# One PSUM tile for all ragged ends: v, k and K tails gathered before a joint transpose, and one sample-output product for both heads

## The chip, the core and the metric

The kernel runs on one core of a Trainium2 chip. The metric is the device time of one execution in microseconds (us). Five engines work side by side, each through its own instructions in order: TensorE (PE in the profile; PEld is its weight load), VectorE (DVE), ScalarE (ACT), GpSimd (POOL) and SyncE (SP), which here issues most of the DMA transfers. They wait for each other by semaphores.

## What is computed

One layer of a decoder: a feed-forward block, a token mixer and a second feed-forward block. 16 meta tokens and 256 prompt tokens (one sequence of 272) and 8 sample tokens (one step of eight independent sequences, each with a state of its own) go through the same weights, so an activation here is a matrix of 280 columns. The mixer, cut to what matters:

```python
q_r, k_r, v_r, g_r, q_h, f_h, i_h, g_h, a_r, a_h = jnp.split(x @ w_in, N_PROJ, axis=-1)
...
# retention, 8 heads of 256 x 256, decay gamma per head
inner = jnp.einsum('bhid,bhjd->bhij', q, k) * D
S_new = jnp.exp(lg * C)[:, None, None] * S + jnp.einsum('bhjd,bhjv->bhdv', k_dec, v)
...
# HGRN2, 16 heads of 128 x 128, gate f per channel, k = 1 - f
A = jnp.einsum('bhid,bhjd,bhijd->bhij', q, k, decay)
o = jnp.einsum('bhij,bhjv->bhiv', A, v) + jnp.einsum('bhid,bhdv->bhiv', q * jnp.exp(b), S)
```

The outputs are y of the prompt and the samples, and both kinds of state after the prompt and after each sample's step.

## The kernel before

Activations lie transposed: 128 channels on the partitions, tokens along the free axis (16 meta, 256 prompt, 8 sample). A product in float32 accuracy is made of three passes in a reduced format: `dense` multiplies the high part of the weights by the high and the low part of x, and the low part of the weights by the high part of x. A weight block of 128x1024 is loaded (`raw`), cast on ACT (`whi`, L187) and subtracted on DVE (`wlo`, L188). The dense matmuls are all L217 in the profile.

The mixer stands between the two feed-forward blocks, from about 780 to 1760 us. It goes through eight units (u = 0 to 7), each with one retention head and two HGRN2 heads, about 130 us for a unit. `project` runs the dense products of `w_in` for the unit's ten projections. After each contraction step it calls `pump`, which advances two generators, `mix_hg` and `mix_ret`. They hold the mixer's own work, cut into steps by `yield n` (come again after n dense steps). TensorE's order is therefore written out by hand: a step's small matmuls stand between dense matmuls, and a matmul whose operand isn't ready holds all dense matmuls behind it. On ACT, DVE and SP a scheduler orders the instructions by priority and estimate. Mixer products take their PSUM bank from a ring of four (`mx_bank`).

The 280 tokens don't fit blocks of 128. Where an operand is needed with tokens on the partitions, it is transposed on TensorE in three pieces, two of 128 tokens and a ragged one. In `mix_ret` (L978 on) the ragged piece has 24 tokens: the prompt's last 16 and the 8 samples. For each half c of the 256 channels, the bank `pt` first takes the three transposes of v (L997). ACT copies out the two whole blocks (`vt`, called vtr in the profile, L998) and the ragged rows (`vt2`, L999). `split` makes the high and low parts `vs`, and `upper_lower_upper` (L705) makes from `vt2` the tile `vs2`: high, low and high parts, 32 rows each, so that one 128-row product does the three passes of the ragged rows. A second bank `pt` takes the transposes of k (L1006), scaled by the decay on ACT (L1011) into `ks` and for the ragged rows into `ks2` (twice), with the low parts subtracted on DVE (L1012). Then the scores `psc` (L1024) follow and, for each c, the prompt state `psr` (L1041): six matmuls of `vs` with `ks`, and as the seventh `vs2` with `ks2`. The profile drops a digit at the end of a name: vs2 and ks2 appear there as vs and ks with 24 rows, vt2 as vt with 24 rows.

The sample rows of `vt2` also leave by a DMA to memory (`vrd`, L720) and come back spread over all partitions (`vbr`, L1055), for the update of the sample states `smr` (L1061).

In `mix_hg` the ragged piece of K is the 16 meta tokens, transposed for each head h into the third part of the bank `ptk` (L899) and split into `km`. The sample outputs of HGRN2 are products of 32 rows each (`pq`, L932), 128 columns for each head. Their result goes through `osh` (L936) and is transposed back per head in `sample_columns` (L727). `alone` (L723) spreads the samples' q columns so that each stands alone in a block of 32 columns.

Of the kernel before, what the change touches and what calls it, by code (L numbers as in the profile page):

```python
# [18 lines left out]
P = 128  # L19
# [31 lines left out]

SCORES = ((0, 0, SEQ, P), (SEQ, P - NMETA, 2 * P - P + NMETA, P), (2 * SEQ - P + NMETA, SEQ - NMETA, NMETA, LP - 2 * P))
# [75 lines left out]
def trunk(ctx: ExitStack, tc: tile.TileContext, A, O):  # L128
# [124 lines left out]
    def sub(out, a, b):  # L253
        nc.vector.tensor_tensor(out=out, in0=a, in1=b, op=ALU.subtract)
# [291 lines left out]
    with tc.tile_pool(name="yp", bufs=1) as yp:  # L546
# [7 lines left out]
        with tc.tile_pool(name="mp", bufs=1) as mp:  # L554
# [33 lines left out]
            qdh = tmp("qdh", (P, 2, NS * 32))  # L588
            qdr = tmp("qdr", (P, 2, NS * 32))
            nc.gpsimd.memset(qdh, 0.0)  # L590
            nc.gpsimd.memset(qdr, 0.0)
            vsm = tmp("vsm", (P, P))
# [8 lines left out]
            sc2 = tmp("sc2", (P, NMETA), dt=F32R)  # L601
            for z in (km, vm, ks2, vs2, sc2):
                z = z if len(z.shape) == 2 else z.rearrange("p c f -> p (c f)")
                nc.scalar.copy(z, qdh[:, 0, : z.shape[1]])
# [106 lines left out]
            def upper_upper_lower(out, x):  # L711
                n = x.shape[0]
                nc.scalar.copy(out[:n], x)
                nc.scalar.copy(out[32 : 32 + n], x)
                sub(out[64 : 64 + n], x, out[:n].bitcast(F32))
# [7 lines left out]
            def alone(qd, q):  # L723
                for e in range(2):
                    nc.vector.tensor_copy(qd[:, :, 128 * e + e : 128 * e + 128 : 32], q[:, :, SEQ + 4 * e : SEQ + 4 * e + 4])

            def sample_columns(on, po, os):  # L727

                nc.tensor.transpose(po[:, 3 * P :], os, ident)
                nc.vector.tensor_copy(  # L730
                    on[:, SEQ:].rearrange("p (e j) -> p e j", e=2), po[:, 3 * P :].rearrange("p (j c) -> p c j", c=32)[:, 0:2, :])

            def mix_hg(u, f, k, q, v):
# [60 lines left out]
                for s in LEVELS:  # L794
# [59 lines left out]
                    if s == 2:  # L854
# [12 lines left out]
                            t4.unsqueeze(3).to_broadcast([P, 2, 16, 8]))  # L867
                    if s in (4, 8):
# [25 lines left out]
                for h in range(2):  # L894
                    kt = tmp("kth", (P, 2, P), bufs=2)
                    kts.append(kt)
                    pt = mx_bank("ptk")
                    for b, (t0, n) in enumerate(((NMETA, P), (NMETA + P, P), (0, NMETA))):
                        nc.tensor.transpose(pt[:n, b * P : (b + 1) * P], K[:, h, t0 : t0 + n], ident)  # L899
                    nc.scalar.copy(kt, pt[:, : 2 * P].rearrange("p (b f) -> p b f", b=2))  # L900
                    upper_upper_lower(km[:, h, :], pt[:NMETA, 2 * P : 3 * P])

                    vb, sm = vbs[h], sms[h]
                    for b in range(NS):
                        nc.scalar.activation(sm[:, b, :], sm[:, b, :], AF.Copy, scale=fk[:, 0, h, b : b + 1])
                        nc.vector.scalar_tensor_tensor(
                            out=sm[:, b, :], in0=vb[:, b, :], scalar=fk[:, 1, h, b : b + 1], in1=sm[:, b, :],
                            op0=ALU.mult, op1=ALU.add)
                    nc.sync.dma_start(O["sgs"][2 * u + h], sm)
                    yield 2  # L910
# [18 lines left out]
                for h in range(2):  # L929
                    for b in range(NS):  # L930
                        j = 32 * (b % 4)
                        nc.tensor.matmul(  # L932
                            pq[j : j + 32, h * P : (h + 1) * P], qdh[:, h, 32 * b : 32 * b + 32], sms[h][:, b, :],
                            start=b < 4, stop=b >= 4, tile_position=(0, j))
                os = tmp("osh", (P, 2 * P))
                nc.scalar.copy(os, pq[:, : 2 * P])  # L936
                yield 4

                def outputs(h):
# [5 lines left out]
                    sample_columns(on[:, h, :], po, os[:, h * P : (h + 1) * P])  # L945
# [31 lines left out]
            def mix_ret(u, q, k, v):  # L977
# [15 lines left out]
                nc.sync.dma_start(dt, A["dtab"][u])  # L993
                for c in range(2):
                    pt = mx_bank("pt")
                    for b, (t0, n) in enumerate(BLOCKS):
                        nc.tensor.transpose(pt[:n, b * P : (b + 1) * P], v[:, c, t0 : t0 + n], ident)  # L997
                    nc.scalar.copy(vt[:, :, c, :], pt[:, : 2 * P].rearrange("p (b f) -> p b f", b=2))  # L998
                    nc.scalar.copy(vt2[:NB, c, :], pt[:NB, 2 * P : 3 * P])  # L999
                    f = slice(c * P, (c + 1) * P)  # L1000
                    split(vs[:, 0, :, f], vs[:, 1, :, f], vt[:, :, c, :])
                    upper_lower_upper(vs2[:, c, :], vt2[:NB, c, :])
                    yield 1
                    pt = mx_bank("pt")
                    for b, (t0, n) in enumerate(BLOCKS):
                        nc.tensor.transpose(pt[:n, b * P : (b + 1) * P], k[:, c, t0 : t0 + n], ident)  # L1006
                    for b, (t0, n) in enumerate(BLOCKS):
                        x, g = pt[:n, b * P : (b + 1) * P], dec[:n, b, u : u + 1]
                        his = [ks[:, 0, b, f]] if b < 2 else [ks2[third[0], c, :], ks2[third[1], c, :]]
                        for hi in his:  # L1010
                            nc.scalar.activation(hi, x, AF.Copy, scale=g)  # L1011
                        nc.vector.scalar_tensor_tensor(  # L1012
                            out=(ks[:, 1, b, f] if b < 2 else ks2[third[2], c, :]), in0=x, scalar=g,
                            in1=his[0].bitcast(F32), op0=ALU.mult, op1=ALU.subtract)
# [54 lines left out]
                for e in range(2):  # L1069
                    for c in range(2):  # L1070
                        for j in range(4):
                            b = 4 * e + j
                            nc.tensor.matmul(
                                pq[32 * j : 32 * j + 32, :256], qdr[:, c, 32 * b : 32 * b + 32],
# [10 lines left out]
                for c in range(2):  # L1085
# [3 lines left out]
                    sample_columns(on[:, c, :], po, os[:, c * P : (c + 1) * P])  # L1089
# [149 lines left out]
```

## Time and profile before

| what | value |
|---|---|
| time, median of 3 runs | 2612.75 us (2611.18 to 2614.51) |
| time of the profiled execution | 2606.34 us |
| its span | 2604.6 us |
| TensorE busy | 99% of the span |
| VectorE, ScalarE, GpSimd busy | 66%, 53%, 0% |
| mean share of the DMA engines, unit u=3 (1140 to 1270 us) | 0.71 |

The profiled execution was 6.4 us under the median of the runs. Between its own time and its span lie 1.74 us. Rows of the trace give the start in us from the start of the span, the duration in us, the engine, the line, the operation, the tiles (output before input) and in brackets the idle time ahead with what ended it. "x3" is three instructions taken as one row. Matmuls are pipelined, so a row's duration is longer than the step from one start to the next, and the step is what a matmul costs.

### The profile page before, as it was taken

Reading aid. Unit: us, or ns where it says so; the run is one execution under the profiler, and the core shown is the slowest. Engines: PE = TensorE matmul, PEld = TensorE weight load, DVE = VectorE, ACT = ScalarE, POOL = GpSimd, SP = SyncE. Lnnn points to the kernel's source line nnn. Section 1 sums busy time; section 2 is a strip of 40 time slices with the busy share of each in tenths; the row PEclk is TensorE's granted clock in tenths of the full one; section 3 lists DMA queues with packets and bytes.
Section 4 is the critical chain, followed back from the end, with each engine's and each line's share of the span. In section 5 each row is a group of like instructions: output and inputs, shape, how many; then the busy total and the mean of one; then the engine's idle time right before and its main releaser. Section 6 shows DMA issues by size and latency. Waiting matters only on the chain.

```text
span 2604.6 us, 54857 instructions
## 1 busy us (share of the span) xinstructions
PE 2581.1 (99%) x22744; PEld 2553.0 (98%) x22744; DVE 1721.4 (66%) x2907; ACT 1380.7 (53%) x2184; POOL 12.1 (0%) x54
## 2 busy tenths in 40 slices
PE   9999999999999999999999999999999999999998
PEld 9999999999999999999999999999999999999998
DVE  6454445565579788777878787776995555556555
ACT  5444444444466667756666666574564444444443
POOL 0000000000000000000000000000000000000000
PEclk9999999999999999999999999999999999999999
DMA  7555555555566686767676767665656566656664
GB/s 243 184 185 186 184 182 186 186 181 184 186 198 217 227 271 211 251 214 248 219 244 213 250 218 244 205 233 194 188 191 198 195 197 196 197 195 194 195 195 147
DMA packets 154586, 536.17 MB, mean 206 GB/s; under 512 B 17696, under 2 KB 25696, under 8 KB 154336
## 3 DMA queue, kind: packets, MB, share of 16 engines
q1 hardware_dynamic: 154048, 532.37, 62.5%
q8 instruction: 178, 2.92, 0.5%
q14 instruction: 72, 0.59, 0.1%
q10 hardware_dynamic: 288, 0.29, 0.1%
HBM read 501.99 MB, written 30.61 MB: 204 GB/s over the span
## 4 chain that ended last, share of the span: by engine, by line
PE 91%; DVE 4%; DMA 2%; ACT 2%; issue 1%; SPq 0%; DVEq 0%; ACTq 0%
PE up L217 36%; PE dn L217 18%; PE wo L217 3%; PE pj_f L217 3%; PE pj_q_h L217 3%; PE pj_g_r L217 3%; PE pj_k_r L217 3%; PE pj_a_r L217 3%; PE pj_v_r L217 3%; PE pj_i_h L217 3%; PE pj_q_r L217 3%; PE pj_g_h L217 3%; PE pj_a_h L217 2%; DVE wlo L188 1%; DMA smr<-in_sr 1%
## 5 line engine op out<-in xcount | busy, mean ns | idle before, releaser
L188 DVE TENSOR_TENSOR wlo<-raw,whi 128x1024 fp32r<-128x1024 f32 (+1 forms) x869 | 1062.6, 1224 | 734.2 <-ACT whi L187 732.4
L187 ACT CAST whi<-raw 128x1024 fp32r<-128x1024 f32 (+1 forms) x870 | 904.9, 1042 | 890.2 <-PE up L217 416.9
L217 PE MATMUL up<-xh,wlo 128*128 128x280 f32 (+1 forms) x2624 | 725.8, 280 | 0.4 <-DVE wlo L188 0.3
L217 PE MATMUL up<-xh,whi 128*128 128x280 f32 (+1 forms) x2624 | 725.7, 280 | 0.5 <-ACT whi L187 0.5
L217 PE MATMUL up<-xl,whi 128*128 128x280 f32 (+1 forms) x2624 | 725.4, 279 | 0.0
L217 PEld LDWEIGHTS up<-xh,wlo 128*128 128x128 f32 x2624 | 492.5, 189 | 1.0 <-DVE wlo L188 1.0
L217 PEld LDWEIGHTS up<-xh,whi 128*128 128x128 f32 x2624 | 492.6, 189 | 0.9 <-ACT whi L187 0.8
L217 PEld LDWEIGHTS up<-xl,whi 128*128 128x128 f32 x2624 | 492.6, 189 | 0.0
L217 PE MATMUL dn<-hh,whi 128*128 128x280 f32 (+1 forms) x1376 | 384.7, 280 | 0.0
L217 PE MATMUL dn<-hh,wlo 128*128 128x280 f32 (+1 forms) x1376 | 384.3, 279 | 0.0
L217 PE MATMUL dn<-hl,whi 128*128 128x280 f32 (+1 forms) x1376 | 384.3, 279 | 0.0
L217 PEld LDWEIGHTS dn<-hh,whi 128*128 128x128 f32 x1376 | 260.1, 189 | 0.1
L217 PEld LDWEIGHTS dn<-hl,whi 128*128 128x128 f32 x1376 | 260.1, 189 | 0.1
L217 PEld LDWEIGHTS dn<-hh,wlo 128*128 128x128 f32 x1376 | 260.1, 189 | 0.0
L217 PE MATMUL pj_g_r<-xh,whi 128*128 128x264 f32 x256 | 76.7, 299 | 0.0
L217 PE MATMUL pj_g_h<-xh,wlo 128*128 128x264 f32 x256 | 71.3, 278 | 3.2 <-DVE wlo L188 3.2
L217 PE MATMUL pj_v_r<-xh,whi 128*128 128x280 f32 x256 | 74.2, 290 | 0.0
L217 PE MATMUL pj_g_h<-xh,whi 128*128 128x264 f32 x256 | 73.6, 287 | 0.0
L217 PE MATMUL pj_k_r<-xh,wlo 128*128 128x280 f32 x256 | 72.6, 283 | 0.2 <-DVE wlo L188 0.2
L217 PE MATMUL pj_v_r<-xh,wlo 128*128 128x280 f32 x256 | 72.4, 283 | 0.3 <-DVE wlo L188 0.3
L217 PE MATMUL pj_k_r<-xh,whi 128*128 128x280 f32 x256 | 72.7, 284 | 0.0
L217 PE MATMUL pj_v_r<-xl,whi 128*128 128x280 f32 x256 | 72.3, 283 | 0.0
(402 smaller groups left out, 5277.6 us busy)
## 6 DMA issues: line engine op xcount, KB each, us to landing
raw<-in_w_up SPq DMA_DIRECT2D x343, 512.0 KB, 3.4
raw<-in_w_in SPq DMA_DIRECT2D x320, 512.0 KB, 3.9
raw<-in_w_dn SPq DMA_DIRECT2D x172, 512.0 KB, 3.6
smr<-in_sr SPq DMA_DIRECT2D x32, 512.0 KB, 5.6
out_srs<-smr SPq DMA_DIRECT2D x32, 512.0 KB, 5.1
raw<-in_w_out SPq DMA_DIRECT2D x32, 512.0 KB, 3.7
smh<-in_sg SPq DMA_DIRECT2D x16, 512.0 KB, 4.2
vbr<-vrd SPq DMA_DIRECT2D x16, 512.0 KB, 4.2
```

The source lines that it names most:

```text
L187: nc.scalar.copy(hi[:, j:jn, :], raw[:, j:jn, :])
L188: nc.vector.tensor_tensor(out=lo[:, j0:j1, :], in0=raw[:, j0:j1, :], in1=hi[:, j0:j1, :].bitcast(F32), op=ALU.subtract)
L217: nc.tensor.matmul(o, w, t, start=start, stop=stop)
```

## The change

The ragged pieces are gathered before they are transposed. GpSimd copies the 24 ragged columns of k and of v, two channel halves each, into one tile `tails` (four groups of 32 columns), and the 16 meta columns of both heads' K into `meta` (two groups of 32). One transpose of `tails` goes into the third part of the bank `pt` of k's first half, and one transpose of `meta` into the bank `ptk` of the first head. In the first, rows 0 to 63 are k and rows 64 to 127 are v: `ks2`, `vt2` and `vs2` for both channel halves are now all read from this one bank. In HGRN2 the sample products of the second head accumulate onto those of the first, in the same 128 columns: the q columns of each sample stand in their own row of the 32, which `alone` now writes with one copy in place of two. `osh` is half as wide, and one transpose and one copy serve both heads.

```diff
+ALONE = 4 * 32 + 1
 SCORES = ((0, 0, SEQ, P), (SEQ, P - NMETA, 2 * P - P + NMETA, P), (2 * SEQ - P + NMETA, SEQ - NMETA, NMETA, LP - 2 * P))
...
-            qdh = tmp("qdh", (P, 2, NS * 32))
-            qdr = tmp("qdr", (P, 2, NS * 32))
+            qdh = tmp("qdh", (P, 4, ALONE))
+            qdr = tmp("qdr", (P, 4, ALONE))
             nc.gpsimd.memset(qdh, 0.0)
             nc.gpsimd.memset(qdr, 0.0)
+            qdh_at = [qdh.rearrange("p a c -> p (a c)")[:, 256 * h :] for h in range(2)]
+            qdr_at = [qdr.rearrange("p a c -> p (a c)")[:, 2 * ALONE * c :] for c in range(2)]
             vsm = tmp("vsm", (P, P))
...
             sc2 = tmp("sc2", (P, NMETA), dt=F32R)
+            tails = tmp("tails", (P, 4, 32))
+            meta = tmp("meta", (P, 2, 32))
+            nc.gpsimd.memset(tails, 0.0)
+            nc.gpsimd.memset(meta, 0.0)
+            dec2 = tmp("dec2", (P, HR))
+            for i in range(2):
+                nc.scalar.copy(dec2[32 * i : 32 * i + T - 2 * P], dec[: T - 2 * P, 2, :])
             for z in (km, vm, ks2, vs2, sc2):
                 z = z if len(z.shape) == 2 else z.rearrange("p c f -> p (c f)")
-                nc.scalar.copy(z, qdh[:, 0, : z.shape[1]])
+                nc.scalar.copy(z, qdh_at[0][:, : z.shape[1]])
             threads = []
...
-            def upper_upper_lower(out, x):
+            def upper_upper_lower(out, x, at=0):
                 n = x.shape[0]
...
                 nc.scalar.copy(out[32 : 32 + n], x)
-                sub(out[64 : 64 + n], x, out[:n].bitcast(F32))
+                sub(out[64 : 64 + n], x, out[at : at + n].bitcast(F32))
...
             def alone(qd, q):
-                for e in range(2):
-                    nc.vector.tensor_copy(qd[:, :, 128 * e + e : 128 * e + 128 : 32], q[:, :, SEQ + 4 * e : SEQ + 4 * e + 4])
+                nc.vector.tensor_copy(
+                    qd[:, :, : 128 : 32].rearrange("p (c e) j -> p c e j", e=2),
+                    q[:, :, SEQ:].rearrange("p c (e j) -> p c e j", e=2))
             def sample_columns(on, po, os):
+                n = on.shape[1]
                 nc.tensor.transpose(po[:, 3 * P :], os, ident)
                 nc.vector.tensor_copy(
-                    on[:, SEQ:].rearrange("p (e j) -> p e j", e=2), po[:, 3 * P :].rearrange("p (j c) -> p c j", c=32)[:, 0:2, :])
+                    on[:, :, SEQ:].rearrange("p h (e j) -> p h e j", e=2),
+                    po[:, 3 * P :].rearrange("p (j c) -> p c j", c=32)[:, : 2 * n, :].rearrange("p (h e) j -> p h e j", e=2))
             def mix_hg(u, f, k, q, v):
...
                             t4.unsqueeze(3).to_broadcast([P, 2, 16, 8]))
+                    if s == 8:
+                        nc.gpsimd.tensor_copy(meta[:, :, :NMETA], K[:, :, :NMETA])
                     if s in (4, 8):
...
                     pt = mx_bank("ptk")
-                    for b, (t0, n) in enumerate(((NMETA, P), (NMETA + P, P), (0, NMETA))):
-                        nc.tensor.transpose(pt[:n, b * P : (b + 1) * P], K[:, h, t0 : t0 + n], ident)
+                    for b in range(2):
+                        t0 = NMETA + b * P
+                        nc.tensor.transpose(pt[:, b * P : (b + 1) * P], K[:, h, t0 : t0 + P], ident)
+                    x = pt[:64, 2 * P : 3 * P]
+                    if h == 0:
+                        nc.tensor.transpose(x, meta.rearrange("p h t -> p (h t)"), ident)
+                        for i in range(2):
+                            upper_upper_lower(km[:, i, :], x[32 * i : 32 * i + NMETA], 32 * i)
                     nc.scalar.copy(kt, pt[:, : 2 * P].rearrange("p (b f) -> p b f", b=2))
-                    upper_upper_lower(km[:, h, :], pt[:NMETA, 2 * P : 3 * P])
...
                         nc.tensor.matmul(
-                            pq[j : j + 32, h * P : (h + 1) * P], qdh[:, h, 32 * b : 32 * b + 32], sms[h][:, b, :],
-                            start=b < 4, stop=b >= 4, tile_position=(0, j))
-                os = tmp("osh", (P, 2 * P))
-                nc.scalar.copy(os, pq[:, : 2 * P])
+                            pq[j : j + 32, :P], qdh_at[h][:, 32 * b : 32 * b + 32], sms[h][:, b, :],
+                            start=h == 0 and b < 4, stop=h == 1 and b >= 4, tile_position=(0, j))
+                os = tmp("osh", (P, P))
+                nc.scalar.copy(os, pq[:, :P])
                 yield 4
...
                         nc.tensor.matmul(o, Ss[h][:, b, :], Q[:, h, b * P : (b + 1) * P], start=False, stop=True)
-                    sample_columns(on[:, h, :], po, os[:, h * P : (h + 1) * P])
+                    if h == 0:
+                        sample_columns(on, po, os)
                     sq = tmp("sqh", (P, TL))
...
                 nc.sync.dma_start(dt, A["dtab"][u])
+                for i, x in enumerate((k, v)):
+                    nc.gpsimd.tensor_copy(tails[:, 2 * i : 2 * i + 2, :NB], x[:, :, 2 * P :])
                 for c in range(2):
                     pt = mx_bank("pt")
-                    for b, (t0, n) in enumerate(BLOCKS):
-                        nc.tensor.transpose(pt[:n, b * P : (b + 1) * P], v[:, c, t0 : t0 + n], ident)
+                    for b in range(2):
+                        nc.tensor.transpose(pt[:, b * P : (b + 1) * P], v[:, c, b * P : (b + 1) * P], ident)
                     nc.scalar.copy(vt[:, :, c, :], pt[:, : 2 * P].rearrange("p (b f) -> p b f", b=2))
-                    nc.scalar.copy(vt2[:NB, c, :], pt[:NB, 2 * P : 3 * P])
                     f = slice(c * P, (c + 1) * P)
                     split(vs[:, 0, :, f], vs[:, 1, :, f], vt[:, :, c, :])
-                    upper_lower_upper(vs2[:, c, :], vt2[:NB, c, :])
                     yield 1
                     pt = mx_bank("pt")
-                    for b, (t0, n) in enumerate(BLOCKS):
-                        nc.tensor.transpose(pt[:n, b * P : (b + 1) * P], k[:, c, t0 : t0 + n], ident)
-                    for b, (t0, n) in enumerate(BLOCKS):
-                        x, g = pt[:n, b * P : (b + 1) * P], dec[:n, b, u : u + 1]
-                        his = [ks[:, 0, b, f]] if b < 2 else [ks2[third[0], c, :], ks2[third[1], c, :]]
+                    for b in range(2):
+                        nc.tensor.transpose(pt[:, b * P : (b + 1) * P], k[:, c, b * P : (b + 1) * P], ident)
+                    if c == 0:
+                        nc.tensor.transpose(pt[:, 2 * P : 3 * P], tails.rearrange("p i t -> p (i t)"), ident)
+                    todo = [(pt[:, b * P : (b + 1) * P], dec[:, b, u : u + 1], [ks[:, 0, b, f]], 0, ks[:, 1, b, f]) for b in range(2)]
+                    if c == 0:
+                        for i in range(2):
+                            r = third[i]
+                            todo.append((pt[r, 2 * P : 3 * P], dec2[r, u : u + 1], [ks2[q, i, :] for q in third[:2]], i, ks2[third[2], i, :]))
+                    for x, g, his, i, lo in todo:
                         for hi in his:
...
                         nc.vector.scalar_tensor_tensor(
-                            out=(ks[:, 1, b, f] if b < 2 else ks2[third[2], c, :]), in0=x, scalar=g,
-                            in1=his[0].bitcast(F32), op0=ALU.mult, op1=ALU.subtract)
+                            out=lo, in0=x, scalar=g, in1=his[i].bitcast(F32), op0=ALU.mult, op1=ALU.subtract)
+                    if c == 0:
+                        for i in range(2):
+                            r = 64 + 32 * i
+                            nc.scalar.copy(vt2[:NB, i, :], pt[r : r + NB, 2 * P : 3 * P])
+                            upper_lower_upper(vs2[:, i, :], vt2[:NB, i, :])
                     yield 2
...
                             nc.tensor.matmul(
-                                pq[32 * j : 32 * j + 32, :256], qdr[:, c, 32 * b : 32 * b + 32],
+                                pq[32 * j : 32 * j + 32, :256], qdr_at[c][:, 32 * b : 32 * b + 32],
                                 sms[2 * e + c][:, j, :], start=e + c == 0, stop=e + c == 2, tile_position=(0, 32 * j))
...
                         nc.tensor.matmul(po[:, l0 : l0 + n], vts[b][:, c, :], scrs[b], start=b == 0, stop=b == 2)
-                    sample_columns(on[:, c, :], po, os[:, c * P : (c + 1) * P])
+                    sample_columns(on[:, c : c + 1, :], po, os[:, c * P : (c + 1) * P])
                     nc.scalar.copy(on[:, c, :SEQ], po[:, :SEQ])
...
```

The code moves the copies of `vt2` and the making of `vs2` from behind each v transpose to behind the first k transpose, and the scheduler places them. Three places follow, with the tiles' full names: ks2, vt2 and vs2 are the ragged ones.

ACT in unit u=3, before, from the first half's `vtr` copy on; whi131 is a weight block's cast:

```order
L998 COPY vtr_14619<-pt_14628 128x2x128
L999 COPY vt2_8636<-pt_14628 24x128
L224 CAST vs_14621<-vtr_14619 128x2x128
L187 CAST whi131_14771<-raw131_14770 128x8x128
L707 CAST vs2_8641<-vt2_8636 24x128
L708 CAST vs2_8641<-vt2_8636 24x128
L1011 ACTIVATE ks_14620<-pt_14645,dec_87 128x128
L998 COPY vtr_14619<-pt_14674 128x2x128
L999 COPY vt2_8636<-pt_14674 24x128
L224 CAST vs_14621<-vtr_14619 128x2x128
L1011 ACTIVATE ks_14620<-pt_14645,dec_87 128x128
L707 CAST vs2_8641<-vt2_8636 24x128
```

The same place now, from the second half's `vtr` copy on:

```order
L1021 COPY vtr_14611<-pt_14674 128x2x128
L225 CAST vs_14613<-vtr_14611 128x2x128
L1037 ACTIVATE ks_14612<-pt_14634,dec_87 128x128
L1037 ACTIVATE ks_14612<-pt_14686,dec_87 128x128
L188 CAST whi132_14842<-raw132_14841 128x8x128
L1037 ACTIVATE ks2_8640<-pt_14634,dec2_8647 24x128 x2
L1037 ACTIVATE ks_14612<-pt_14686,dec_87 128x128
L1037 ACTIVATE ks2_8640<-pt_14634,dec2_8647 24x128 x2
L887 COPY acch_14083<-pl_14726 64x2x64 x2
L1043 COPY vt2_8636<-pt_14634 24x128 x2
L717 CAST vs2_8641<-vt2_8636 24x128
L718 CAST vs2_8641<-vt2_8636 24x128
```

Behind these come two more casts into vs2 and the sro copy of the first state. The copies into vt2 and the casts into vs2 stood ahead of the ks2 activations and among them; now they stand behind the last ks2 activation and the two acch copies, as the last work ahead of sro.

DVE in unit u=3, before, from the second half's `vs` subtraction; cen and vtr are the centring of v's rows, wlo132 a weight block:

```order
L225 TENSOR_TENSOR vs_14621<-vtr_14619,vs_14621 128x2x128
L254 TENSOR_TENSOR vs2_8641<-vt2_8636,vs2_8641 24x128
L1012 SCALAR_TENSOR_TENSOR ks_14620<-pt_14691,dec_87,ks_14620 128x128
L974 TENSOR_SCALAR cen_14809<-cen_14809 128x2
L975 TENSOR_TENSOR vtr_14619<-vtr_14619,cen_14809 128x512
L188 TENSOR_TENSOR wlo132_14853<-raw132_14851,whi132_14852 128x8x128
L1012 SCALAR_TENSOR_TENSOR ks2_8640<-pt_14645,dec_87,ks2_8640 24x128
```

DVE now, from the second half's `ks` subtraction; dtab is the masking of the scores:

```order
L1038 SCALAR_TENSOR_TENSOR ks_14612<-pt_14686,dec_87,ks_14612 128x128
L995 TENSOR_SCALAR cen_14799<-cen_14799 128x2
L996 TENSOR_TENSOR vtr_14611<-vtr_14611,cen_14799 128x512
L189 TENSOR_TENSOR wlo132_14843<-raw132_14841,whi132_14842 128x8x128
L1038 SCALAR_TENSOR_TENSOR ks2_8640<-pt_14634,dec2_8647,ks2_8640 24x128
L1038 SCALAR_TENSOR_TENSOR ks_14612<-pt_14686,dec_87,ks_14612 128x128
L240 TENSOR_TENSOR dtab_14618<-psc_14714,dtab_14618 128x400
L1038 SCALAR_TENSOR_TENSOR ks2_8640<-pt_14634,dec2_8647,ks2_8640 24x128
```

The subtraction into vs2 (L254, now L255) is gone from here and stands behind the products K and Q that follow; the second ks2 subtraction comes right behind dtab.

ACT in unit u=1, before, from a weight cast on; smh are the sample states of HGRN2's second head:

```order
L187 CAST whi57_11392<-raw57_11391 128x8x128
L224 CAST vs_11128<-vtr_11126 128x2x128
L1011 ACTIVATE ks2_8640<-pt_11177,dec_87 24x128 x2
L707 CAST vs2_8641<-vt2_8636 24x128
L708 CAST vs2_8641<-vt2_8636 24x128
L1011 ACTIVATE ks_11127<-pt_11217,dec_87 128x128
L905 ACTIVATE smh_11448<-smh_11448,fk_10840 128x128 x5
L1011 ACTIVATE ks_11127<-pt_11217,dec_87 128x128
L905 ACTIVATE smh_11448<-smh_11448,fk_10840 128x128
```

ACT in unit u=1 now, from the same weight cast on:

```order
L188 CAST whi57_11392<-raw57_11391 128x8x128
L1037 ACTIVATE ks_11128<-pt_11176,dec_87 128x128
L1037 ACTIVATE ks_11128<-pt_11222,dec_87 128x128
L925 ACTIVATE smh_11448<-smh_11448,fk_10842 128x128 x3
L1037 ACTIVATE ks2_8640<-pt_11176,dec2_8647 24x128 x2
L1037 ACTIVATE ks_11128<-pt_11222,dec_87 128x128
L925 ACTIVATE smh_11448<-smh_11448,fk_10842 128x128
L1037 ACTIVATE ks2_8640<-pt_11176,dec2_8647 24x128 x2
L188 CAST whi58_11422<-raw58_11421 128x8x128
L1043 COPY vt2_8636<-pt_11176 24x128 x2
L717 CAST vs2_8641<-vt2_8636 24x128
```

Three smh activations now stand ahead of the first ks2 activation, where five stood behind it, and a weight cast stands between the last ks2 activation and the vt2 copies.

## The prediction

> **What bounds the kernel now.** The page comes first: who is busy, and which engine the chain that ended last runs through.
>
> ```profile
> PE 2581.1 (99%) x22744; PEld 2553.0 (98%) x22744; DVE 1721.4 (66%) x2907; ACT 1380.7 (53%) x2184; POOL 12.1 (0%) x54
> PE 91%; DVE 4%; DMA 2%; ACT 2%; issue 1%; SPq 0%; DVEq 0%; ACTq 0%
> ```
>
> TensorE is busy for 99% of the span and carries 91% of the chain. So each matmul slot taken away shortens the time, and each microsecond in which TensorE waits lengthens it. The list of TensorE's waits shows which ones exist.
>
> ```profile
> PE psr L1041 <- DVE ks L1012: 3.6, 3, 2.4
> PE pj_g_h L217 <- DVE wlo L188: 3.2, 6, 0.8
> PE pt L1006 <- DVE acch L805: 1.5, 1, 1.5
> ```
>
> The first is the place that the change rebuilds: the first state product waits for the ragged low part of ks, in three of the eight units. In the other five it doesn't wait. How near they are to it decides this case, so the timeline of a steady unit is read next, engine by engine.
>
> **What a transpose costs.** TensorE's timeline around one group of three:
>
> ```profile
> 1046.99 0.28 PE L217 MATMUL pj_a_r<-xh,wlo 128*128 128x264 f32 x1
> 1047.10 0.49 PE L997 MATMUL pt<-ident,v 128*128 128x128 f32 x3
> 1047.35 0.36 PE L217 MATMUL pj_g_r<-xh,whi 128*128 128x264 f32 x1
> 1047.55 0.28 PE L217 MATMUL pj_g_r<-xl,whi 128*128 128x264 f32 x1
> 1047.66 0.28 PE L217 MATMUL pj_g_r<-xh,wlo 128*128 128x264 f32 x1
> ```
>
> A dense matmul steps by 0.11 us (1047.55 to 1047.66). From 1046.99 to 1047.55 pass 0.56 us with two dense matmuls, so three transposes take 0.56 - 0.22 = 0.34, that is 0.11 us each. Each unit loses five of them: the ragged pieces of v (two), of k's second half, of K's second head, and one of osh. The ones that stay move 128 columns as before. 8 x 5 x 0.11 = **4.4 us less** on the engine that bounds. The `pq` products keep their number.
>
> The removed work elsewhere (one of two `alone` copies, half of osh, one copy of sample columns per unit) lies on DVE and ACT, at 66% and 53% busy, and isn't counted. The 24 GpSimd copies are new. The nearest rows are the engine's own 32-column copies:
>
> ```profile
> L737 POOL COPY ends<-v x8: 352/972/1482, 798.5 to 1660.3; 128x32 f32<-128x32 f32 x8
> L738 POOL COPY ends<-v x8: 202/205/205, 800.0 to 1661.2; 128x32 f32<-128x32 f32 x8
> ```
>
> They take 0.2 to 1.5 us, on an engine that is idle. v is complete before its own transposes, and the tails are needed a dense step or more behind these, so I count nothing; were the cover gone, it would be up to 1 us in a unit.
>
> **What is moved.** All five operands of the ragged product now come from one bank, and the order places vt2 and vs2 last. This is unit u=3 before:
>
> ```profile
> 1179.52 0.25 ACT L999 COPY vt<-pt 24x128 f32<-24x128 f32 x1
> 1180.89 0.30 ACT L708 CAST vs<-vt 24x128 fp32r<-24x128 f32 x1
> 1181.73 1.03 ACT L187 CAST whi<-raw 128x1024 fp32r<-128x1024 f32 x1
> 1182.78 0.75 ACT L1011 ACTIVATE ks<-pt,dec 24x128 fp32r<-24x128 f32 x2
> 1184.90 0.73 ACT L1011 ACTIVATE ks<-pt,dec 24x128 fp32r<-24x128 f32 x2 [1.37 <-DVE ks L1012]
> 1185.66 0.53 ACT L872 COPY acch<-pl 64x128 f32<-64x128 f32 x2
> 1181.50 0.28 DVE L254 TENSOR_TENSOR vs<-vt,vs 24x128 fp32r<-24x128 f32 x1
> 1182.28 0.69 DVE L975 TENSOR_TENSOR vtr<-vtr,cen 128x512 f32<-128x512 f32 x1
> 1182.89 1.22 DVE L188 TENSOR_TENSOR wlo<-raw,whi 128x1024 fp32r<-128x1024 f32 x1
> 1184.14 0.73 DVE L1012 SCALAR_TENSOR_TENSOR ks<-pt,dec,ks 24x128 fp32r<-24x128 f32 x2
> 1184.69 0.94 PE L1041 MATMUL psr<-vs,ks 128*128 128x256 f32 x7
> 1186.82 0.94 PE L1041 MATMUL psr<-vs,ks 128*128 128x256 f32 x7
> ```
>
> Before, vs2 was ready at 1181.8 (1181.50 + 0.28), and psr's seventh matmul needed beside it only the first ks2, at 1184.5 (1184.14 + 0.36, half of the pair). psr began at 1184.69: 0.2 us to spare, the seventh matmul having six times 0.11 more. The second ks2 was due only for the second psr at 1186.82.
>
> Now the seventh matmul of the first psr needs both halves of vs2 whole, and they come behind this chain. Let E be the end of the first ks2 subtraction. Then in ACT's order: two ks2 activations of the second channel half (0.73), two acch copies (0.53), two vt2 copies (0.16 for the first, by the step of such a copy to the next instruction, 0.25 for the last), four casts (three steps of 0.32 and 0.30). This sums to 2.9 us. DVE's vs2 subtraction (0.28) runs beside the last cast. The ACT row above with 1.37 us idle shows that ACT waits for DVE between reads of one bank. By the Trainium skill, page "PSUM — Partial Sum Buffer", section "PSUM bank collisions raise a hardware error", two engines must not be in one bank and 32-partition quadrant at once, reads included, and the scheduler adds a dependency for it: that speaks against gathering the tails in one bank, and the 1.37 us agree with it.
>
> E moves too. DVE and ACT lose the work of vs2 and vt2 ahead of the weight block: on DVE two subtractions of 0.28, on ACT the casts and copies (six of 0.16 to 0.32, about 1.5 us) that it waited for. I put wlo 1.0 us earlier, so E = 1183.5 in place of 1184.5 (at the least 0.0, at the most 1.4 earlier). vs2 is then ready at 1186.4. TensorE is three transposes (0.33) earlier at psr, 1184.36, and free for the seventh at 1184.36 + 6 x 0.11 = 1185.0. It **waits 1.3 us** (0.9 to 2.3). Nothing else covers that: all dense matmuls stand behind. Five units are of this kind (u=2 to 6): +6.5 us (4.5 to 11.5).
>
> Unit u=0 waits already, and so long that its clock falls:
>
> ```profile
> 830.52 1.86 PE L1041 MATMUL psr<-vs,ks 128*128 128x256 f32 x7 [2.44 <-DVE ks L1012]
> 833.34 0.40 PE L217 MATMUL pj_f<-xh,wlo 128*128 128x280 f32 x1
> 833.58 0.28 PE L217 MATMUL pj_f<-xh,whi 128*128 128x280 f32 x1
> ```
>
> Behind the 2.44 us dense matmuls step by 0.23 in place of 0.12 until 833.58. The 3.06 us from 830.52 hold 13 matmuls that take 1.5 at full clock: 1.6 us lost. The new wait falls into the same place as the old. I count 0 (-0.9 to +1.0). The Trainium skill, page "TensorE: Matmul & The Clock Gate", Part 1, has a free-running window of 3.4 us, in which an idle engine loses half its clock; the stretch at half clock here fits that length, but 2.44 us of idling were enough.
>
> Unit u=1 has another order: three smh activations ahead of the first ks2, whose states come by DMA, and a weight cast ahead of vt2.
>
> ```profile
> 937.31 0.94 PE L1041 MATMUL psr<-vs,ks 128*128 128x256 f32 x7
> 941.76 0.38 PE L1041 MATMUL psr<-vs,ks 128*128 128x256 f32 x1 [0.97 <-DVE ks L1012]
> 931.44 0.39 SPq L757 DMA_DIRECT2D smh<-in_sg  x1
> smh<-in_sg SPq DMA_DIRECT2D x16, 512.0 KB, 4.2
> 936.76 1.56 ACT L905 ACTIVATE smh<-smh,fk 128x128 f32<-128x128 f32 x5
> 939.04 1.04 ACT L187 CAST whi<-raw 128x1024 fp32r<-128x1024 f32 x1
> ```
>
> The states land at 931.44 + 0.3 + 4.2 = 935.9. Then on ACT three smh (0.3 each), two ks2, the wait for DVE's subtraction, ks, smh, two ks2, the cast (1.0), two vt2 and four casts: 0.9 + 0.7 + 0.35 + 0.3 + 0.7 + 1.0 + 0.4 + 1.25 = 5.6, with a wait or two 6.0. The seventh matmul runs at 941.9, where TensorE would be free at 937.6: 4.3 us of waiting, of which the 0.97 at 941.76 goes away. Counted against before, 3.2 us more. The gap is longer than that of u=0, so I add its 1.6 us at half clock: +4.8 (1.6, if the states are early, to 6).
>
> Unit u=7 has meta's casts and a weight cast on ACT ahead of the first head's kth copy, and psr already waits 0.23 us:
>
> ```profile
> 1706.42 1.52 PE L1024 MATMUL psc<-q_r,k_r 128*128 128x256 f32 x8
> 1709.52 1.05 PE L1041 MATMUL psr<-vs,ks 128*128 128x256 f32 x7 [0.23 <-DVE ks L1012]
> ```
>
> psc takes the bank of the ring of four that this kth copy must have left. I put that behind the weight cast (1.04) and a ragged cast or two, 1.2 us late, and the seventh matmul behind its vs2 casts as in u=3, 0.7 more: +1.9 (0.5 to 2.5).
>
> Sum: -4.4 + 6.5 + 0 + 4.8 + 1.9 = +8.8. While TensorE waits, DVE gets ahead, and of the 3.2 us that pj_g_h waits for wlo about a third goes: -1. **+7.8 us.** The profiled execution (2606.34, the span and 1.74 around it) would go to 2614.1; it lay 6.4 under the median, and the median 2612.75 goes to **2620.6 us**. All low ends together (-4.4 + 4.5 - 0.9 + 1.6 + 0.5 - 2) give -0.7, all high ends (-4.4 + 11.5 + 1 + 6 + 2.5) +16.6.
>
> **The rivals.** A measurement here tells 0.2% (5.2 us) from no change.
>
> *The transposes alone count.* Here the weight block isn't held at its present place: ACT and DVE, freed of the copies and casts, start it 2.4 us earlier, E is 1182.1, and vs2 is ready at 1185.0 when TensorE comes. No steady unit waits, the wait and the half clock in u=0 shrink (1.4 and 1.6), and u=1 and u=7 take their low ends: -4.4 - 3.0 + 1.6 + 0.5 - 1 = -6.3, 2606.5. For it: ACT and DVE are little more than half busy, and E needs only 1.0 to 1.4 us beyond what I give it. Against it: 2.9 us of ACT work stand behind E in the written order, which no row makes shorter, and the weight cast of 1181.73 has no idle time ahead of it that could be used. This is the rival on the other side; it decides if E comes before 1182.1 in u=3. Chance 0.11.
>
> *Stalls and savings balance.* The steady wait is 0.9, and u=1 doesn't lose its clock: -4.4 + 4.5 + 3.2 + 0.5 - 1 = +2.8, 2615.6. Chance 0.24.
>
> *The sample rows come late.* vt2 leaves for memory 5.3 us later than now, behind its last copy (1179.77 to about 1185.1).
>
> ```profile
> 1180.00 0.33 SPq L720 DMA_DIRECT2D vrd<-vt  x1
> 1183.04 0.33 SPq L1055 DMA_DIRECT2D vbr<-vrd  x1
> 1187.56 1.28 DVE L1061 SCALAR_TENSOR_TENSOR smr<-vbr,k_r,smr 128x256 f32<-128x256 f32 x3
> 1188.75 1.22 DVE L188 TENSOR_TENSOR wlo<-raw,whi 128x1024 fp32r<-128x1024 f32 x1
> ```
>
> vbr then starts at 1188.2 and lands 4.2 later (as smh of the same size), 1192.5. DVE waits there in its order, with the weight block wlo behind smr: three smr and a wlo, 1.28 + 1.22, end at 1195. I put TensorE's need of that block at 1196.8. If the block is needed 2 us earlier than I read it, the unit loses up to 2 us more, in seven units 8 to 14: 2629 to 2635. Chance 0.14.
>
> **How the numbers follow.** My forecast (waits of 0.9 to 2.3 in each steady unit, total +5.2 to +14) has 0.51; the rivals 0.11, 0.24 and 0.14. The range 2609 to 2630 leaves out most of the first rival and half of the third. Faster by over 0.2% (below 2607.5) is most of the first rival: 0.09. Same is the rest of it and the second: 0.26. Slower is my forecast and the third: 0.65.
>
> **What would show it.** Right: 40 rows of transposes and osh fewer; psr's row split in six and one in units 2 to 6, the one with 0.9 to 2.3 us of idle time ended by ACT's or DVE's vs2; in u=1 a wait of some 4 us and a stretch at half clock behind it. Wrong: psr still as one row of seven without idle time, or waits of TensorE at wlo behind smr.

## The result, and the profile after

The changed kernel takes 2625.55 us (median of 6 runs, 2623.53 to 2631.34), the kernel before 2612.45 (6 runs, 2610.72 to 2617.19): 13.1 us more, a ratio of 1.0051 with a 95% interval of 1.0041 to 1.0061. The profiled execution took 2624.16 us with a span of 2622.4, 17.8 us more than that of before, which was one of the shortest of its kernel.

The page's first and fourth part, in the changed kernel:

```profile
PE 2586.8 (99%) x22704; PEld 2556.3 (97%) x22704; DVE 1721.1 (66%) x2883; ACT 1386.5 (53%) x2186; POOL 27.1 (1%) x80
PE 89%; DVE 5%; ACT 3%; DMA 2%; issue 1%; SPq 0%; DVEq 0%; ACTq 0%
```

The 40 matmuls are gone (22744 to 22704), and DVE and ACT have a larger share of the chain. TensorE's waits:

```profile
PE psr L1071 <- ACT vs L718: 7.7, 5, 1.5
PE psr L1071 <- DVE vs L255: 4.9, 2, 4.5
PE pj_g_h L218 <- DVE wlo L189: 4.3, 7, 0.8
PE psr L1071 <- DVE ks L1038: 2.0, 1, 2.0
PE psc L1054 <- ACT kth L921: 1.9, 1, 1.9
```

psr waited 3.6 us in all, and now 14.6. In five units the last vs2 cast on ACT ends it, in u=1 DVE's vs2. Unit u=3, on three engines:

```profile
1195.65 0.83 PE L1071 MATMUL psr<-vs,ks 128*128 128x256 f32 x6
1198.02 0.35 PE L1071 MATMUL psr<-vs,ks 128*128 128x256 f32 x1 [1.54 <-ACT vs L718]
...
1194.81 0.73 ACT L1037 ACTIVATE ks<-pt,dec 24x128 fp32r<-24x128 f32 x2 [0.96 <-DVE ks L1038]
1195.57 0.53 ACT L887 COPY acch<-pl 64x128 f32<-64x128 f32 x2
1196.05 0.55 ACT L1043 COPY vt<-pt 24x128 f32<-24x128 f32 x2
1197.58 0.30 ACT L718 CAST vs<-vt 24x128 fp32r<-24x128 f32 x1
...
1194.43 0.72 DVE L1038 SCALAR_TENSOR_TENSOR ks<-pt,dec,ks 24x128 fp32r<-24x128 f32 x2
```

psr's row of seven is split into six and one. The seventh stands until the cast of 1197.58 is done. It costs more than the idle time shows: from the sixth start (five steps of 0.11 behind 1195.65, so 1196.20) to 1198.02 pass 1.82 us in place of 0.11, so 1.7 us. From the dense matmul ahead of psr to the one behind it, it is 2.66 us (1195.54 to 1198.20) in place of 0.89.

A second loss is in no list of waits. The samples' products pqr fill TensorE in four column groups at once, and where one group waits, the row only gets longer. The groups of lines, before and after, and the last unit's rows, before and after:

```profile
L1073 PE MATMUL pqr<-smr,qdr 128*32 128x256 f32 x256 | 16.2, 382 | 0.0
L1103 PE MATMUL pqr<-smr,qdr 128*32 128x256 f32 x256 | 19.6, 383 | 0.0
1733.62 1.89 PE L1073 MATMUL pqr<-smr,qdr 128*32 128x256 f32 x29
1752.22 3.37 PE L1103 MATMUL pqr<-smr,qdr 128*32 128x256 f32 x29
```

3.4 us more of busy time in all, 1.5 of it in u=7. In time, from the dense matmul ahead to the one behind, units 1 to 7 lost 3.4 us more and u=0 1.1 less. In u=3 itself pqr lost nothing (2.29 us before, 1.89 now). What it waits for is in DVE's waits for the sample rows (before and after), in DVE's smr rows of u=7 (two before, one after), and in SP's rows of u=3, which show how late the rows leave:

```profile
DVE smr L1061 <- DMA vbr<-vrd: 16.5, 8, 3.4
DVE smr L1091 <- DMA vbr<-vrd: 28.1, 15, 3.7
1729.53 1.67 DVE L1061 SCALAR_TENSOR_TENSOR smr<-vbr,k_r,smr 128x256 f32<-128x256 f32 x4 [3.36 <-DMA vbr<-vrd]
1732.25 1.67 DVE L1061 SCALAR_TENSOR_TENSOR smr<-vbr,k_r,smr 128x256 f32<-128x256 f32 x4
1751.66 3.25 DVE L1091 SCALAR_TENSOR_TENSOR smr<-vbr,k_r,smr 128x256 f32<-128x256 f32 x8 [3.66 <-DMA vbr<-vrd]
1196.62 0.29 SPq L730 DMA_DIRECT2D vrd<-vt  x1
1199.20 0.42 SPq L1085 DMA_DIRECT2D vbr<-vrd  x1
```

In u=7 four of the eight smr were done before pqr began, and the last ended 0.3 us behind its start (1733.9 and 1733.6); now the last ends 2.7 us behind it (1754.9 and 1752.2). In u=3 vt2 leaves right behind its last copy. Against psr's start that is 0.97 us later (1196.62 and 1195.65); it was 4.69 us earlier (1180.00 and 1184.69).

Unit u=1 and the clock:

```profile
945.37 0.55 PE L1071 MATMUL psr<-vs,ks 128*128 128x256 f32 x1 [4.50 <-DVE vs L255]
945.71 0.43 PE L218 MATMUL pj_g_r<-xh,whi 128*128 128x264 f32 x1
948.78 0.43 PE L218 MATMUL pj_a_r<-xh,wlo 128*128 128x264 f32 x1
949.00 0.85 PE L1071 MATMUL psr<-vs,ks 128*128 128x256 f32 x3
```

Behind the 4.50 us dense matmuls step by 0.22 (948.78 to 949.00) in place of 0.11. The granted clock (the share of TensorE's full clock, by the profile) was 0.50 from 943.24, inside the wait, to 950.07, and 1.00 behind that.

### The profile page after: what moved, and what is told of

It reads as the page before. It is cut to its first block, busy times and chain, and to the rows that moved or that the text cites. A ratio compares the mean times of both kernels' runs of the same rounds, so it can differ in the third digit from the quotient of the medians.

```text
span 2622.4 us, 54813 instructions
## 1 busy us (share of the span) xinstructions
PE 2586.8 (99%) x22704; PEld 2556.3 (97%) x22704; DVE 1721.1 (66%) x2883; ACT 1386.5 (53%) x2186; POOL 27.1 (1%) x80
## 4 chain that ended last, share of the span: by engine, by line
PE 89%; DVE 5%; ACT 3%; DMA 2%; issue 1%; SPq 0%; DVEq 0%; ACTq 0%
PE up L218 36%; PE dn L218 18%; PE pj_v_r L218 3%; PE wo L218 3%; PE pj_f L218 3%; PE pj_k_r L218 3%; PE pj_q_h L218 3%; PE pj_i_h L218 3%; PE pj_q_r L218 3%; PE pj_g_r L218 3%; PE pj_g_h L218 3%; PE pj_a_h L218 3%; PE pj_a_r L218 3%; DVE wlo L189 2%; DMA smr<-in_sr 1%
## 5 line engine op out<-in xcount | busy, mean ns | idle before, releaser
L218 PE MATMUL pj_k_r<-xl,whi 128*128 128x280 f32 x256 | 72.5, 283 | 0.0
```

What stands on the lines that cost most here:

```text
L218: nc.tensor.matmul(o, w, t, start=start, stop=stop)
```

## Experiments

Each ratio is against the kernel before, run on the same chip at the same time. The kernels are edits of the changed kernel, and short diffs show them.

**The HGRN2 half alone (e7_hg_only).** `mix_ret` as before, `mix_hg` as changed.

> Only the HGRN2 half: meta and the joint product of the samples; v and k transposed with their own 24-row pieces as before. Theory: 16 transposes of 0.11 us go (-1.8), psr doesn't wait in units 2 to 6, and u=7 pays for kth behind the weight cast (+2 to +2.5): 2612 to 2614. Rival (transposes alone count, u=7's wait belongs to the tails): 2610.5 to 2611.5.

Ratio 0.9999 (0.9990 to 1.0008). psc waits 1.4 us for kth in u=7, and psr in units 2 to 6 doesn't wait. Of the 1.8 us that 16 transposes save, the one wait takes most back: this half changes nothing that the measurement can tell.

**The retention half alone (e6_ret_only).** `mix_hg` as before.

> Only the retention half of the change: tails for v and k; HGRN2 with its own 16-row transposes and one product and one osh half per head, as before. Theory: all waits of psr and pqr stay, 16 transposes of 0.11 us come back (+1.8), and the psc wait of 1.9 us in u=7 goes with half of what follows (-2 to -3): 2623 to 2625.5. Rival (the two halves matter only together, through the load on ACT): 2617 to 2621.

Ratio 1.0059 (1.0044 to 1.0073); 2627.76 us, above what either theory gave. pqr lost still more than in the changed kernel (20.9 us busy and 1.1 idle), and in u=0 the half clock lasted 6.8 us in place of 3.4; that these two make up the rest is not shown. The loss lies wholly in this half.

**The sample rows freed (e2_rows_apart).**

```diff
+            vraw = tmp("vraw", (P, 2, P))
...
+                    if c == 0:
+                        for i in range(2):
+                            r = 64 + 32 * i
+                            nc.scalar.copy(vraw[:NB, i, :], pt[r : r + NB, 2 * P : 3 * P])
                     todo = [(pt[:, b * P : (b + 1) * P], ...
...
-                vrow = rows_out(vt2.rearrange("p c f -> p (c f)")[16:24, :], 256, "vr")
+                vrow = rows_out(vraw.rearrange("p c f -> p (c f)")[16:24, :], 256, "vr")
```

> Only the sample rows are freed: an extra early copy of the ragged v rows (two ACT copies per unit more) feeds the DMA to vrd, while vt2 and vs2 stay last as in the changed kernel. Theory: psr still waits about 1.7 us in units 2 to 6 (0.3 more by the two added copies), and the wait of pqr for the last smr goes, from 4.1 us summed over the units to below 1: 2622 to 2625. Rival (pqr is late for another reason, DVE being pushed back by the psr waits): pqr's extra stays and the time is 2625 to 2628.

Ratio 1.0030 (1.0021 to 1.0039), 2619.3 us: better than forecast. Lines and DVE's wait in this kernel:

```profile
L1108 PE MATMUL pqr<-smr,qdr 128*32 128x256 f32 x256 | 15.5, 381 | 0.0
L1076 PE MATMUL psr<-vs,ks 128*128 128x256 f32 x112 | 18.0, 292 | 18.3 <-DVE vs L255 8.6 <-ACT vs L719 7.7 <-DVE ks L1043 2.0
DVE smr L1096 <- DMA vbr<-vrd: 10.0, 6, 2.2
```

pqr loses nothing any more (19.6 to 15.5), though psr waits longer than in the changed kernel: 7.7 us in the steady units as there, and 7.1 in u=1, where the vt2 copies fell behind four smh activations. The ratio is 0.0021 below the changed kernel's 1.0051, about 5 us, while psr waits 3.7 us more: late sample rows are a cost of their own, and not a small one.

**vt2 and vs2 written first (e1_v_first).** The block that makes them, moved ahead of `todo`.

> The joint transposes stay, but the two vt2 copies and the making of vs2 are written ahead of the ks and ks2 work of the same bank. Theory (order): the time was lost because vs2 and vt2 come last on ACT. Then psr in units 2 to 6 no longer waits (5 x 1.7 us), the 4.7 us gap of u=1 goes with its half clock, the waits of pqr for smr go (3.4 us), and about 2 us in u=7 (psc waits for kth) stay: 2625.5 - 8.5 - 4.5 - 3.4 = 2609, within 2607 to 2612. Rival (one bank): the reads of one bank by two engines one after the other are the cost, in whatever order; the ks2 work is then 1.5 us later by the copies and casts put ahead of it, and psr waits 1 to 1.5 us in each unit: 2617 to 2622.

Ratio 1.0008 (0.9998 to 1.0018), 2614.04 us. By the ratios 11 of the 13 us come back by the order alone, by the medians (2614.04 and 2610.22) 9. The theory's 2609 was not reached. psr still waits, now for ks2, which the copies and casts push back:

```profile
1187.68 1.05 PE L1071 MATMUL psr<-vs,ks 128*128 128x256 f32 x7 [0.48 <-DVE ks L1043]
```

So the rival has a part in it: reading one bank for all, something has to be last.

**psr later (e4_psr_later).** Both psr products two dense steps later: `yield 2` ahead of them to `yield 4`, `yield 18` behind them to `yield 16`.

> The changed kernel with both psr products two dense steps (about 1.35 us) later, and the long pause behind them two steps shorter, so that pqr keeps its place. Theory: the wait of the seventh matmul is plain lateness of vs2, and shrinks by what TensorE comes later: from 1.7 to about 0.35 in units 2 to 6 (-6.8 us) and from 4.7 to 3.3 in u=1; pqr's waits stay at about 4 us: 2616 to 2619, 1.002 to 1.0035 of before. Rival (the wait moves along, since ACT's order moves with psr): 2622 to 2626.

Ratio 1.0066 (1.0054 to 1.0078), 2627.99 us: slower than either text gave, and the theory missed on psr in the steady units and on pqr.

```profile
L1103 PE MATMUL pqr<-smr,qdr 128*32 128x256 f32 x256 | 31.0, 412 | 3.7 <-DVE smr L1091 3.7
L1071 PE MATMUL psr<-vs,ks 128*128 128x256 f32 x112 | 17.0, 281 | 8.9 <-ACT vs L718 5.2 <-DVE vs L255 3.1 <-DVE ks L1038 0.6
1195.28 0.30 ACT L717 CAST vs<-vt 24x128 fp32r<-24x128 f32 x1
1195.49 1.04 ACT L188 CAST whi<-raw 128x1024 fp32r<-128x1024 f32 x1
1196.55 0.29 ACT L718 CAST vs<-vt 24x128 fp32r<-24x128 f32 x1
```

The wait of the five steady units falls from 7.7 only to 5.2 in sum, as the scheduler put a weight cast of 1.04 us between the casts into vs2. And the smr updates, written behind psr, come later for a pqr that kept its place: 31.0 us in place of 19.6.

**A bank of its own (e11_own_bank).**

```diff
-                        nc.tensor.transpose(pt[:, 2 * P : 3 * P], tails.rearrange("p i t -> p (i t)"), ident)
+                        pv = mx_bank("ptt")
+                        nc.tensor.transpose(pv[:, :P], tails.rearrange("p i t -> p (i t)"), ident)
```

The reads go to `pv`; vt2 and vs2 are still written last.

> One thing changed against the changed kernel: the joint transpose of the tails writes a PSUM bank of its own from the ring of four, in place of the third part of the bank of k's first half. The code that makes vt2 and vs2 is still written last. Theory (the shared bank made ACT's and DVE's reads wait for each other, and so put vt2 and vs2 last): the seventh psr matmul no longer waits in units 2 to 6 (-8.5 us), the gap of u=1 falls from 4.7 us to below 1.5, pqr's waits from 4.1 to 1 to 3 us, u=7's psc wait for kth stays at about 2: 2609 to 2613, 0.9995 to 1.001 of before. Rival (the place in the code is what counts): psr waits stay above 1 us, 1.003 or more. Rival (a fifth bank for a ring of four): new waits of 0.5 us or more at the next transposes or psc, 1.002 or more.

Ratio 1.0029 (1.0020 to 1.0038). TensorE's waits and groups:

```profile
PE pj_g_h L218 <- DVE wlo L189: 6.1, 8, 0.8
PE ptt L1030 <- ACT vtr L1021: 2.4, 1, 2.4
PE psc L1055 <- ACT vt L1044: 1.2, 1, 1.2
L1072 PE MATMUL psr<-vs,ks 128*128 128x256 f32 x112 | 15.5, 276 | 0.5 <-ACT ks L1038 0.5
```

psr's waits fall from 14.6 to 0.5 us by the bank alone, with the code in the same order. vt2 and vs2 still come behind the ks2 work on ACT, but in u=3 vs2 is ready 0.3 us ahead of psr's start, where it came 2.2 us behind it: sharing the bank with k's blocks is what made them late when they are written last. But the second rival holds as well: the ring has to give a fifth bank, and the joint transposes (0.7 us in u=0, 2.4 in u=1) and psc (0.9 in u=0, 1.2 in u=7) wait. These 5.2 us aren't the whole of what was lost. TensorE also waits 3.7 us at pl in u=0 and 1.9 at ptk in u=1 for K from DVE, pqr takes 20.3 us and 2.7 of idle time, and pj_g_h waits 6.1. Which of these follow from the ring isn't shown.

With the rows written first and kth ahead of km as well (e12_own_bank_rows):

> Candidate: own bank as in e11_own_bank, the two vt2 copies and the DMA to vrd written first behind the transposes, and kth ahead of km in HGRN2. Theory: psr waits gone, pqr's waits gone (the sample rows leave as early as in the kernel before), psc's wait in u=7 gone: the 4.4 us of the transposes remain, 0.9975 to 0.999 of before. Rival (pqr and wlo, both behind DVE, wait whatever is done for the rows): 0.9995 to 1.001.

Ratio 1.0022 (1.0014 to 1.0031): the rival's direction, and beyond its range. pqr came back to 16.9 us busy, which again points to the late rows; the joint transposes still waited 2.2 us, psc 1.4 and pj_g_h 6.2.

**Tails in the bank of v's second half (e3_v_bank),** one step ahead of the last k transposes, with vt2 and vs2 made right behind the vtr copy, and kth ahead of km. These are three edits at once, and the ratio doesn't tell them apart.

```diff
+                    if c == 1:
+                        nc.tensor.transpose(pt[:, 2 * P : 3 * P], tails.rearrange("p i t -> p (i t)"), ident)
                     nc.scalar.copy(vt[:, :, c, :], pt[:, : 2 * P].rearrange("p (b f) -> p b f", b=2))
```

> The joint transpose of the tails goes into the bank of v's second half (one step ahead of the last k transposes) instead of that of k's first half, so vt2, vs2 and ks2 are read from a bank whose other reader is only vtr; in HGRN2 the kth copy is written ahead of the km casts. Theory (the order and the place of the ragged reads cost the time, the transposes saved are worth 0.11 us each): no wait at the seventh psr matmul in units 2 to 6, none at psc in u=7, pqr's waits at the level of the kernel before (0.5 to 2 us): the 4.4 us of the transposes remain, 0.998 to 1.000 of the kernel before. Rival (the gathering itself costs: GpSimd's copies late for the transpose, a bank held longer in the ring of four): new waits at the transposes in each unit, 1.001 to 1.003.

Ratio 0.9994 (0.9986 to 1.0003), as the theory said, though not clear of no change, and pqr did not come to the level of the kernel before (20.0 us busy). Then with the two vt2 copies and the DMA to vrd ahead of that vtr copy (e8_rows_first):

> Candidate: e3_v_bank with the two vt2 copies and the DMA to vrd written ahead of the vtr copy. Theory: pqr's extra, 5.4 us summed over the units in e3_v_bank, falls below 2 us, since the rows leave about 1 us earlier: 0.998 to 0.9993 of before, 1 to 3 us below e3_v_bank. Rival (pqr is late through DVE's load, not through the rows): as e3_v_bank, 0.9994 within 0.0008.

Ratio 0.9987 (0.9978 to 0.9996), 2607.47 us against 2610.71: 3.2 us less, and the one version that is clear of the kernel before. Its interval overlaps that of e3_v_bank; what the rows bring is read from pqr, 20.0 to 15.6 us.

```profile
L1107 PE MATMUL pqr<-smr,qdr 128*32 128x256 f32 x256 | 15.6, 382 | 0.0
L1075 PE MATMUL psr<-vs,ks 128*128 128x256 f32 x112 | 15.8, 281 | 5.9 <-DVE dtab L240 3.5 <-DVE ks L1048 1.5 <-ACT kth L919 0.9
```

pqr loses nothing, and psr waits 5.9 us for other things, most of it for dtab. Two tries to cover such a wait by a later psr failed. The first starts from e1_v_first (e5_v_first_kth_later):

> Candidate: vt2 and vs2 ahead of ks as in e1_v_first, kth ahead of km, psr one dense step later. Theory: the 0.65 us that psr still waited in units 2 to 6 are covered by the later place (3.3 us less than e1_v_first), psc's 2.3 us in u=7 go: 0.998 to 1.000 of the kernel before. Rival (pqr and wlo waits take the gain back, as DVE is the next in line): 1.000 to 1.002.

Ratio 1.0025 (1.0016 to 1.0034). psr's waits went from 5.1 to 1.3 us, and pqr rose from 17.4 to 21.0 busy. The second starts from e8_rows_first (e13_rows_first_later):

> e8_rows_first with the two psr products one dense step (0.68 us) later, and all that follows with them. In e8_rows_first psr still waits 0.7 us in units 2 to 6, for dtab, whose bank it takes. Theory: the step covers that wait, the rows that leave early keep pqr without waits: 3 us less than e8_rows_first, 0.997 to 0.9985 of before. Rival (as in e4_psr_later and e5_v_first_kth_later, what DVE does behind psr comes later, and wlo or smr wait instead): 0.9985 to 1.0005.

Ratio 1.0018 (1.0007 to 1.0029). Its waits:

```profile
PE pj_f L218 <- DVE wlo L189: 5.3, 11, 0.6
PE pj_g_h L218 <- DVE wlo L189: 5.1, 8, 0.8
```

psr's waits went (5.9 to 1.4), and 5.3 us of waiting for weight blocks came at pj_f, where e8_rows_first had 0.4. DVE's work behind psr came later with it, which is the rival's account; it ended beyond the rival's range as well.

**The kernel before, once more (e0_before_again).**

> The kernel before a second time, for its trace alone: which of its waits repeat. All theories: the psr waits (2.4 in u=0, about 1 in u=1, 0.2 in u=7) repeat within 0.3 us; the waits of pj_g_h for wlo (3.2 in the first trace, 4 to 6 in the others) vary from run to run by 2 us or more, without any change of the kernel.

2608.26 us. Its waits for wlo at pj_g_h were 2.5 (3.2 in the first trace): they did not vary by 2 us, so the theory missed there. u=0's psr wait repeated (2.4), u=1's of 0.97 did not: there psr didn't wait. Over the versions the waits at pj_g_h are 2.3 (e4_psr_later) and 2.5 (e2_rows_apart) to 6.3 us; with one trace of each, what part belongs to a version stays open. The two traces also tell how far a single unit can be read: by dense matmuls, this one is some 3.5 us longer in u=0 and u=1 together, and some 2 shorter in units 2 to 7.

## Why the prediction was right or wrong

The forecast was +7.8 us, 2620.6 within 2609 to 2630, with slower at 0.65; measured +13.1, 2625.55. The direction, the main mechanism and its place were right, the size too small. By the trace's stages, dense matmul against dense matmul: u=0 +3.2, u=1 +4.2, units 2 to 6 +8.6, u=7 +2.5 us. These add up to 18.5 and not to 13.1, since the trace of before was 6 us under its median; against its second trace u=0 and u=1 together are some 3.5 us less.

- *The transposes.* 0.11 us each, as forecast: groups of two in the changed kernel, such as that of 1057.00, push the dense matmuls by 0.22 where groups of three pushed them by 0.33.

```profile
1056.89 0.28 PE L218 MATMUL pj_a_r<-xh,wlo 128*128 128x264 f32 x1
1057.00 0.38 PE L1020 MATMUL pt<-ident,v 128*128 128x128 f32 x2
1057.14 0.36 PE L218 MATMUL pj_g_r<-xh,whi 128*128 128x264 f32 x1
1057.34 0.28 PE L218 MATMUL pj_g_r<-xl,whi 128*128 128x264 f32 x1
```

- *The steady wait:* 1.7 for 1.3. (The prediction's own figures give 1.4: 2.93 behind E, less the 0.86 and six steps of 0.11.) E came 0.86 us ahead of psr (1194.43 + 0.36, and 1195.65), the very distance forecast (1183.5 and 1184.36). The term mis-sized was the ACT tail behind it: 3.1 us (to 1197.88) for 2.9, the two vt2 copies taking 0.55 for 0.41, and 0.14 from the last cast to the matmul, which was not counted. With the slip of 0.1 that is 2 us in five units.
- *The sample rows* were the third rival at 0.14, and given as hidden in the forecast. This is the step that failed: the price was put on wlo behind smr, and the slack taken to cover it. The cost showed at pqr, which in the kernel before had next to no slack either (from the dense matmul ahead of it to the one behind it, 2.54 and 2.33 us in u=3 and u=4, and 2.14 where nothing waits). +3.4 us of busy time, and in e2_rows_apart they were gone.
- *wlo.* I took 1 us off for DVE getting ahead. Its waits at pj_g_h grew instead, 3.2 to 4.3. That DVE stood waiting for the rows, with the weight block queued behind them, would fit, and with the rows freed they were 2.5 (e2_rows_apart). But with the rows late they were 2.3 in e4_psr_later, and with the rows early 4.4 in e8_rows_first, so the cause isn't shown.
- *u=1:* +4.8 less its five transposes is +4.25, and +4.2 came, with the wait (4.50) and the half clock that were forecast. That the size agrees so well is in part luck, as the second trace of the kernel before shows (the 0.97 that was taken off didn't come there). By the Trainium skill, page "TensorE: Matmul & The Clock Gate", Part 1, the clock goes by a free-running window of 3.4 us; the stretches at half clock agree with that, 3.42 us (830.15 to 833.57, in u=0 before) and 6.83 (943.24 to 950.07 here), one window and two. Behind the wait TensorE worked at half clock for 4.7 us (945.37 to 950.07), where the price of 1.6 us came from 3.1 in u=0. The waits of 1.54 in the steady units left the clock whole.
- *u=0* was held at no change, and lost 3.2: a wait of 1.9 us at pl for K that DVE had late, and a stretch at half clock (881.80 to 885.22, behind waits of 0.72 and 0.90 us at pvr), less 1.1 at pqr. I had not followed DVE's order beyond psr there.
- *u=7:* +2.5 for 1.9 less 0.55. psc waited for kth, as forecast, but 1.9 us for 1.2, and the clock fell behind it (0.50 from 1724.89 to 1728.31), which was not in the sum. The 0.7 at the seventh matmul didn't come: psr ran without a wait. 1.5 of u=7 is pqr. That the sum is near is luck.
- *The rival on the other side* (E early enough) is refuted for this kernel: E was where the forecast put it.
- *Stalls and savings balance* is refuted too: the steady wait was 1.7 and not 0.9, and u=1 lost its clock.

What stays open: which part of the loss with a bank of its own (1.0029, and 1.0022 with the rows first) is the ring and which is DVE's order, since both moved; and what sets the waits at pj_g_h.

## What to carry to other kernels

Before merging small pieces into one PSUM bank to save instructions, list who reads that bank and who needs each read first: here the readers of the shared bank came one after the other, and TensorE waited for the last. Five savings of 0.11 us in a unit were lost to a single wait of 1.7. Give the merged piece a place where its bank has few other readers, and let what leaves by DMA go first, since the round trip through memory had next to no slack here.

## What the runs showed of the hardware

The stretches at half clock between 780 and 1760 us were 3.4 us long or a multiple of it in every trace: 3.42 (u=0 before), 6.83 (943.24 to 950.07, around the wait of 4.50 us) and 10.24 (942.55 to 952.79, around the wait of 7.1 us in e2_rows_apart). Each of these two began inside its wait. The length of a shorter wait doesn't decide by itself: 1.92 us at psc in u=7 were followed by half clock (from 1724.89), 1.87 at pl in u=0 were not, nor were 2.51 at pl in e3_v_bank, nor the waits of 1.54.

And a matmul in a column group of 32 that waits need not show as idle time of TensorE: pqr's 3.4 us appear as busy time alone. Where all groups wait, idle time shows too (in e4_psr_later 3.7 us beside 31.0 busy).
